# The opening of a diffusion trunk on one core: products of ones on TensorE, the first token half first in the DMA queue, another chain to the first norm, and both up-weights of block 1 as plain products

## The chip, the cores and the metric

One NeuronCore of a Trainium2 chip runs the whole program, in one launch. The engines are TensorE (PE, with its weight loads as PEld), VectorE (DVE), ScalarE (ACT), GpSimd (POOL) and SyncE (SP, whose queue issues most of the DMAs). The metric is the device time of one execution in microseconds (us); the time of a kernel is the median of several executions.

## The reference

One layer of a trunk on 640 tokens (512 latent, 128 context) of width 1024: half a SwiGLU feed-forward step, a token mixer (differential attention beside an mLSTM), and a second half feed-forward step. Each is preceded by an RMS norm whose scale and shift come from a conditioning vector (adaLN). The change touches only what comes first:

```python
def adaln(cvec, w, b):
    m = jax.nn.silu(cvec) @ w + b
    return m.reshape(cvec.shape[0], N_MOD, D_MODEL)

def swiglu(h, w1, w3, w2):
    return (jax.nn.silu(h @ w1) * (h @ w3)) @ w2

def layer(x, mods, l, p, ctx):
    m = [mods[:, j][:, None, :] for j in range(N_MOD)]
    g = p['g_norm'][l]
    hh = rmsnorm(x, g[0]) * (1 + m[1]) + m[0]
    x = x + 0.5 * m[2] * swiglu(hh, p['ffn1_w1'][l], p['ffn1_w3'][l], p['ffn1_w2'][l])
    ...
```

Everything is float32. D_FF is 2816, that is 11 blocks of 256 columns for `ffn1_w1` and `ffn1_w3`.

## The kernel before, in words

**Tiling.** Activations are kept transposed: 128 partitions x 8 slices d of the width x 640 tokens, and the tokens in two halves of 320 (half 0, half 1). A float32 product is made of three faster ones (`mm3`): weight and activation are each split into a high part, rounded to fp32r, and a low part, the remainder; high x high, high x low and low x high are added in PSUM. So a weight tile costs ACT a copy (the high part) and DVE a subtraction (the low part). A unit, 128 features x 320 tokens, is 8 slices x 3 = 24 matmuls of 128x320. Float32 matmuls that are not split show as two instructions each.

**Opening** (lines 751 to 919). `x` of half 0 is loaded in two parts (`load_x`), then the adaLN weights `w_ada_k` one k at a time (`start.load(k)`, 1 MB, four buffers, so that load k+4 waits for product k), and in between the weights W of block 0 in four pieces (`load_weights(i)`, `w1a` and `w3a`, slices 2i and 2i+1). `squares` squares x on ACT and DVE and adds pairs on DVE; `add_squares` sums over partitions by a matmul with `ones`; `rstd` and `refine` make the reciprocal root (`rv`, `rt`, `ry`; ACT does a logarithm and an exponential, DVE a Newton step). `product(k)` is a vector-matrix product of the conditioning with `w_ada_k` (16 matmuls into `ps_a`, a copy of the row to SBUF), `columns(k)` turns the row into columns (`ps_at`) and adds the bias and forms `scale`. `divide` multiplies x by the reciprocal root, `norm` applies scale and shift and splits the result into `hm`.

**First pass, second pass.** Then come 8 steps over k for half 0: step k makes 12 matmuls (two weights x two feature tiles x three products) into four accumulators (`ps_f`). Between its first 4 and the other 8 matmuls, `ahead` brings columns k+1, divide, norm of d=k+1 and the splits of W; behind the step stands product k+2. Squares, sum and `rstd` of half 1 are spread over steps 1 to 5. The second pass is 8 steps over half 1.

**Order.** In the opening each engine works as written (`keep_in_program_order`): PE, ACT, DVE and the DMAs on SP's queue each in the order of the program text. Behind the second pass a planner of the framework orders DVE and ACT by a simulated timeline, except where `tc.issue_after` binds an instruction to another one. PE stays in the order written. DMAs of one queue are issued in order, and an issue can wait for an earlier landing.

**Blocks 1 to 10.** A granule is one of `w1`, `w3` of one block. The first granule, `w1` of block 1, is computed plainly (`Whole`: `split` and 4 units, 96 matmuls). All others go through a seven-product scheme over 2x2 blocks (`Winograd.products`): 7 products of 4 slices x 3 matmuls, 84 in all, from sums of weights and of activations. `operand_sums` makes the activation sums once (S1 to S4, DVE and ACT; the low parts of S3 come by `third`, S4 by `fourth`). Per granule, `parts` makes weight parts (`wB`, `wC`, differences in `raw`) and `sums` splits what is left (`ww`). Raw weights have two buffers (`rawp`); the `w` ring for split weights has two. Products A22 and S4 of a granule are made during the next one. `modulation` hangs other work (column tiles of the rest of adaLN) on the granules by number.

Of the kernel before, what the change touches and what calls it, by code (L numbers as in the profile page):

```python
# [21 lines left out]
HALF = T // 2  # L22
# [9 lines left out]
def tile_trunk(ctx: ExitStack, tc: tile.TileContext, a: dict):  # L32
# [83 lines left out]
    cT = load(cp, [128, KT, 2], a["cT"], name="cT")  # L116
# [4 lines left out]
    for r in range(2):  # L121
        load_x(0, r)
    sel = cp.tile([128, 2], F32, name="sel")
# [123 lines left out]
    class Granule:  # L247
# [12 lines left out]
        def parts(self, fp):  # L260
# [12 lines left out]
            tt(vec, lo[:, nk:], lo[:, nk:], hi[:, nk:], ALU.subtract)  # L273
# [40 lines left out]
    class Winograd:  # L314
# [61 lines left out]
        def products(self, work, between, then=(), ahead=None, prepared=False, narrow=0):  # L376
# [356 lines left out]
    with ExitStack() as ph:  # L733
# [11 lines left out]
        class Opening:  # L745
# [8 lines left out]

            def squares(self, hf, r):
# [8 lines left out]
                tt(vec, p, p, q, ALU.add)  # L764
                self.sq[r] = p
                if r == 0:
                    order, psum.order = psum.order, [7]
                    self.ss[hf] = psum.tile([128, 512], F32, tag="mm", name="ps_ss")[:, :HALF]
                    psum.order = order

            def add_squares(self, hf, r):
                for i in range(2):
                    mm(self.ss[hf], ones, self.sq[r][:, i], start=r + i == 0, stop=r + i == 2)
# [14 lines left out]
            def divide(self, hf, r):  # L788
                xs = x_all[:, 2 * r : 2 * r + 2, half(hf)]
                tt(vec, xs, xs, self.rs[hf][:, None, :].to_broadcast([128, 2, HALF]), ALU.mult)  # L790

            def product(self, k):
# [9 lines left out]
                placed(vec.tensor_copy(self.row[k], ps[:, :256]))  # L802
# [32 lines left out]
        def split_weights(i, part):  # L835
            cs = slice(256 * PIECES[i][0], 256 * PIECES[i][1])
            for raw, (h, lo) in zip(raws, W):
# [93 lines left out]
        for k in range(KT):  # L931
# [5 lines left out]
            if k == 5:  # L937
                whole.split(t=[((0, 2048, w1[0]),), ((0, 1792, w1[1]), (1792, 2048, w1[2][:, :256]))])
# [10 lines left out]
        for f, hf in ((0, 1), (1, 1), (0, 0), (1, 0)):  # L949
            p = acc_tile(psum)  # L950
            for k in range(KT):
                mm3(p, whole.w(0, k, f), whole.w(1, k, f), *hs.hh(k, hf), k == 0, k == KT - 1)
            gate_first(f, hf, p, None)
# [1382 lines left out]
```

## Time and profile before

| | us |
|---|---|
| median of 3 executions | 1838.76 |
| lowest and highest | 1837.59, 1839.71 |
| profiled execution | 1840.36 |
| its span, first to last instruction | 1838.6 |

Mean granted TensorE clock of the profiled execution: 0.993 of full speed.

How to read it: a row of the timeline has start, duration, engine, line, operation, tiles (out<-in), shape and count, and in brackets the idle time of the engine before it with what ended it. Many instructions are made in helpers, so the line is that of the helper (75 for matmuls, 51 for ACT, 54 for DVE, 97 for DMAs) and the tile name tells what it is. The granted clock is what the throttle of TensorE allowed. The duration of a matmul in the profile is longer than its spacing from the next, since matmuls overlap. `128x320 f32` stands in the profile for fp32r matmuls too. SPq is SP's queue, on which DMAs are issued.

### The profile page before, as it was taken

How to read it: one execution, taken by the hardware profiler on the slowest of the kernel's cores; microseconds unless marked ns; L12 is line 12 of the kernel's file. 1: busy time of each engine (PE TensorE's matmuls, PEld its weight loads, DVE VectorE, ACT ScalarE, POOL GpSimd, SP SyncE). 2: the span in 40 equal slices, each digit the busy share in tenths (PEclk: the TensorE clock that was granted, in tenths of full speed). 3: DMA queues.
4: the chain of work that ended last, by engine and by line, in shares of the span. 5: the costliest groups of instructions: out<-in, count | busy, mean ns of one | idle time of the engine just before them, and what ended most of it. 6: DMA issues, size and time to landing. Idle time of an engine off the chain costs nothing.

```text
span 1838.6 us, 30679 instructions
## 1 busy us (share of the span) xinstructions
PE 1799.5 (98%) x12608; PEld 1761.4 (96%) x12608; DVE 1317.2 (72%) x2148; ACT 867.7 (47%) x1490; POOL 31.0 (2%) x55
## 2 busy tenths in 40 slices
PE   7999999999999999999999999999899999999999
PEld 5999999999999999999999999999899999999999
DVE  5898886577787757475585558876766878887575
ACT  4654454112655555454465555673235645554232
POOL 0000001110000000000000000000000000000000
PEclk8999999999999999999999999999999999999999
DMA  7354547975234322122222154574742345447872
GB/s 289 121 192 169 193 169 250 370 239 176 72 122 145 122 81 79 63 85 67 77 77 84 41 168 147 199 268 164 257 174 86 132 149 188 166 170 254 322 286 87
DMA packets 127709, 298.77 MB, mean 162 GB/s; under 512 B 9617, under 2 KB 90769, under 8 KB 114769
## 3 DMA queue, kind: packets, MB, share of 16 engines
q1 hardware_dynamic: 118306, 256.44, 40.1%
q0 software_dynamic: 9264, 40.37, 6.0%
q8 instruction: 99, 1.62, 0.4%
q14 instruction: 40, 0.33, 0.1%
HBM read 233.15 MB, written 63.63 MB: 161 GB/s over the span
## 4 chain that ended last, share of the span: by engine, by line
PE 84%; DVE 6%; DMA 5%; ACT 3%; issue 1%; SPq 0%; DVEq 0%; ACTq 0%
PE ps_f L75 45%; PE ps_p L75 16%; PE ps_t L75 11%; PE sc L75 3%; PE ps_o L75 2%; PE ps_n L75 2%; DMA ada<-csil_dram 2%; DVE ww L54 1%; PE ps_u L75 1%; PE ps_wT L78 1%; DMA raw_a<-in_w_ada_c 1%; PE ps_qkT L78 1%; DVE raw_a L716 1%; ACT wH L51 1%; PE ps_ss L75 1%
## 5 line engine op out<-in xcount | busy, mean ns | idle before, releaser
L75 PE MATMUL ps_f<-S,ww 128*128 128x320 f32 x2172 | 350.2, 310 | 5.8 <-DVE ww L54 4.2
L75 PEld LDWEIGHTS ps_f<-S,ww 128*128 128x128 f32 x2172 | 327.0, 189 | 8.5 <-DVE ww L54 6.9
L75 PE MATMUL ps_p<-hH,wH 128*128 128x320 f32 x672 | 213.4, 318 | 6.9 <-DVE y L54 6.2
L75 PE MATMUL ps_p<-hL,wH 128*128 128x320 f32 x672 | 208.2, 310 | 0.0
L75 PE MATMUL ps_p<-hH,wL 128*128 128x320 f32 x672 | 208.2, 310 | 0.0
L51 ACT ACTIVATE ww<-raw 128x2048 fp32r<-128x2048 f32 (+1 forms) x67 | 125.6, 1874 | 154.9 <-PE ps_f L75 87.6
L75 PE MATMUL ps_f<-hm,ww 128*128 128x320 f32 x1236 | 195.6, 311 | 2.5 <-DVE ww L54 2.5
L75 PEld LDWEIGHTS ps_f<-hm,ww 128*128 128x128 f32 x1236 | 185.8, 189 | 2.8 <-DVE ww L54 2.8
L75 PE MATMUL ps_t<-wH,hH 128*128 128x256 f32 x640 | 185.3, 289 | 0.9 <-DVE x L57 0.9
L75 PE MATMUL ps_t<-wH,hL 128*128 128x256 f32 x640 | 181.1, 283 | 0.9 <-DVE hL L54 0.9
L75 PE MATMUL ps_t<-wL,hH 128*128 128x256 f32 x640 | 180.9, 283 | 0.0
L54 DVE TENSOR_TENSOR ww<-raw,ww 128x2048 fp32r<-128x2048 f32 (+1 forms) x67 | 150.1, 2240 | 38.7 <-ACT ww L51 38.7
L75 PE MATMUL ps_f<-hm,wB 128*128 128x320 f32 x984 | 157.6, 309 | 0.0
L75 PEld LDWEIGHTS ps_f<-hm,wB 128*128 128x128 f32 x984 | 147.7, 188 | 0.0
L54 DVE TENSOR_TENSOR raw<-raw 128x1024 f32<-128x1024 f32 x159 | 137.6, 865 | 2.0
L75 PEld LDWEIGHTS ps_p<-hH,wH 128*128 128x128 f32 x672 | 126.9, 189 | 7.6 <-ACT wH L51 6.4
L75 PEld LDWEIGHTS ps_p<-hL,wH 128*128 128x128 f32 x672 | 126.9, 189 | 0.3
L75 PEld LDWEIGHTS ps_p<-hH,wL 128*128 128x128 f32 x672 | 126.7, 189 | 0.0
L54 DVE TENSOR_TENSOR wL<-raw,wH 128x2048 fp32r<-128x2048 f32 x43 | 98.3, 2286 | 35.6 <-ACT wH L51 35.6
L75 PEld LDWEIGHTS ps_t<-wH,hH 128*128 128x128 f32 x640 | 122.4, 191 | 1.5 <-ACT nsq L51 1.1
L75 PEld LDWEIGHTS ps_t<-wH,hL 128*128 128x128 f32 x640 | 122.4, 191 | 1.1 <-DVE hL L54 1.1
L75 PEld LDWEIGHTS ps_t<-wL,hH 128*128 128x128 f32 x640 | 122.5, 191 | 0.4
(303 smaller groups left out, 3353.7 us busy)
## 6 DMA issues: line engine op xcount, KB each, us to landing
g_dram<-g SPq DMA_DIRECT2D x44, 640.0 KB, 5.6
raw_a<-in_w_ada_c SPq DMA_DIRECT2D x24, 512.0 KB, 4.0
raw<-in_w1b SPq DMA_DIRECT2D x11, 1024.0 KB, 4.8
raw<-in_w3b SPq DMA_DIRECT2D x11, 1024.0 KB, 4.8
raw<-in_w1a SPq DMA_DIRECT2D x10, 1024.0 KB, 4.8
raw<-in_w3a SPq DMA_DIRECT2D x10, 1024.0 KB, 6.2
ada<-in_w_ada_c POOLq DMA_DIRECT2D x18, 512.0 KB, 5.0
hm<-g_dram POOLq DMA_DIRECT2D x7, 1280.0 KB, 10.5
```

The lines of the kernel that those rows point to most:

```text
L51: return placed(nc.scalar.activation(*args, **kw))
L54: return placed(eng.tensor_tensor(out=out, in0=in0, in1=in1, op=op))
L75: tc.keep_in_program_order(nc.tensor.matmul(*args, **kw))
L78: tc.keep_in_program_order(nc.tensor.transpose(*args, **kw))
L716: placed(vec.tensor_tensor_reduce(out=junk, in0=raw, in1=self.csil[:, v, :], op0=ALU.mult, op1=ALU.add, scale=1.0, scalar=0.0, accum_out=m ...
```

## The change

1. A method `keep_clock(n)` issues n matmuls of `ones` with `ones` (128x128, float32) into a PSUM bank that nothing reads; it is called with 14 ahead of everything else on PE, and with 3, 4 and 2 between the steps of the opening.
2. `cT`, the conditioning, is loaded by ACT's queue instead of SP's. On SP's queue W piece 0 goes ahead of load 0, x of half 1 goes behind load 5, and W pieces 2 and 3 go behind loads 4 and 6.
3. For half 0 the squares are not added in pairs across ACT and DVE: DVE adds its own two, and `ones` is multiplied with three tiles for each part instead of two.
4. W piece 0 is split ahead of `rstd`, the row of product 0 is copied by ACT, the first divide covers one slice of d only, and norm of d=0 goes ahead of product 1.
5. Squares of half 1 both stand behind step 3, their sums behind step 4, `refine` of half 1 in step 6.
6. `w3` of block 1 is computed plainly as well, from the `w` ring; the seven-product scheme begins at block 2. Parts of the second of its granules are bound ahead of `third`.

```diff
-    cT = load(cp, [128, KT, 2], a["cT"], name="cT")
+    cT = cp.tile([128, KT, 2], F32, name="cT")
...
+    nc.scalar.dma_start(out=cT, in_=a["cT"])
...
             if ahead is not None:
                 with tc.issue_after(work[0][0].split_at):
-                    behind = ahead()
+                    work[1][0].parts(self.fp)
+                with tc.issue_after(work[1][0].parts_at):
+                    ahead()
...
-                if not last:
-                    with tc.issue_after(behind if i == 0 and ahead is not None else gr.split_at):
+                if not last and (i > 0 or ahead is None):
+                    with tc.issue_after(gr.split_at):
                         work[i + 1][0].parts(self.fp)
...
+            def keep_clock(self, n):
+
+                if not hasattr(self, "idle"):
+                    self.idle = self.bank(3, "ps_idle")
+                for _ in range(n):
+                    mm(self.idle[:, :128], ones, ones, start=True, stop=True)
...
-                tt(vec, p, p, q, ALU.add)
-                self.sq[r] = p
+                if hf:
+                    tt(vec, p, p, q, ALU.add)
+                    self.sq[r] = p[:, 0], p[:, 1]
+                else:
+                    tt(vec, q[:, 0], q[:, 0], q[:, 1], ALU.add)
+                    self.sq[r] = p[:, 0], p[:, 1], q[:, 0]
...
-                placed(vec.tensor_copy(self.row[k], ps[:, :256]))
+                if k == 0:
+                    act(self.row[k], ps[:, :256], AF.Copy)
+                else:
+                    placed(vec.tensor_copy(self.row[k], ps[:, :256]))
...
         start = Opening()
+        load_weights(0)
         start.load(0)
         for t, n in ((sel, "sel"), (b_ada, "b_ada"), (g_norm, "g_norm")):
             dma(t, a[n])
-        load_weights(0)
         start.load(1)
         start.load(2)
-        load_x(1, 0)
         load_weights(1)
         start.load(3)
-        load_x(1, 1)
-        load_weights(2)
 
         psum.order = [4, 5, 6]
-        for r in range(2):
-            start.squares(0, r)
-            start.add_squares(0, r)
+        start.keep_clock(14)
+        start.squares(0, 0)
+        start.add_squares(0, 0)
+        start.squares(0, 1)
+        split_weights(0, "high")
+        split_weights(0, "low", slice(1))
+        start.add_squares(0, 1)
+        start.rstd(0)
+        split_weights(0, "low", slice(1, 2))
         start.product(0)
         start.load(4)
-        load_weights(3)
-        start.rstd(0)
-        split_weights(0, "high")
+        load_weights(2)
+        start.keep_clock(3)
         start.refine(0)
         start.columns(0)
-        start.divide(0, 0)
+        start.keep_clock(4)
+        start.divide(0, 0, 1)
+        start.norm(0, 0)
         start.product(1)
-        split_weights(0, "low")
-        start.norm(0, 0)
+        start.divide(0, 0, 1, 1)
         start.load(5)
+        load_x(1, 0)
+        load_x(1, 1)
+        start.keep_clock(2)
...
-                if k == 5:
+                if k == 6:
                     start.refine(1)
...
+                if k == 0:
+                    load_weights(3)
-            if k in (3, 4):
-                start.add_squares(1, k - 3)
-            if k in (1, 2):
-                start.squares(1, k - 1)
+            if k == 3:
+                for r in range(2):
+                    start.squares(1, r)
             if k == 4:
+                for r in range(2):
+                    start.add_squares(1, r)
                 start.rstd(1)
...
-        _, _, gate_first, _ = hs.work.pop(0)
-        whole = Whole(4, hs.up[0].fetch)
-        whole.load()
-        hs.up[1].load()
+        gated = [hs.work.pop(0)[2] for _ in range(2)]
+        whole = [Whole(4, gr.fetch) for gr in hs.up[:2]]
+        for w in whole:
+            w.load()
...
+        whole_units(whole[0], gated[0], ((0, 1), (1, 1), (0, 0), (1, 0)))
         with tc.issue_after(end.ins), tc.issue_after(at_act.ins):
             third, fourth = hs.operand_sums(lambda r: x_all[:, 2 * r : 2 * r + 2, :])
+        whole[1].split()
+        hs.up[3].load()
+        hs.store_g(hs.SO, 0)
+        whole_units(whole[1], gated[1], ((0, 0), (1, 0), (0, 1), (1, 1)))
         with tc.issue_after(end.ins), tc.issue_after(at_act.ins):
             hs.work[0][0].parts(fp)
             hs.work[0][0].sums()
-        hs.store_g(hs.SO, 0)
...
-                if (i, at) == (1, 1):
+                if (i, at) == (2, 1):
                     begin_columns()
-                if at and 2 <= i < 16:
+                if at and 3 <= i < 17:
                     columns.tile(hs.at_vec)
...
-        hs.run_whole(resid, half_m[:, 0], to_mixing, lambda i, at: modulation(i + 1, at), third)
+        hs.run_whole(resid, half_m[:, 0], to_mixing, lambda i, at: modulation(i + 2, at), third)
```

`whole_units` holds the loop of four units that stood in line before, `mm3` over 8 slices and then the gate. `bank` takes a PSUM tile from a named bank.

More of the change, by code (lines that the diff above doesn't have):

```diff
@@ L763, in squares @@
                 tt(vec, q, xs[:, 2:4], xs[:, 2:4], ALU.mult)
-                tt(vec, p, p, q, ALU.add)
-                self.sq[r] = p
+                if hf:
[4 more added lines that the diff above has]
+                    self.sq[r] = p[:, 0], p[:, 1], q[:, 0]
                 if r == 0:
-                    order, psum.order = psum.order, [7]
-                    self.ss[hf] = psum.tile([128, 512], F32, tag="mm", name="ps_ss")[:, :HALF]
-                    psum.order = order
+                    self.ss[hf] = self.bank(7, "ps_ss")[:, :HALF]
             def add_squares(self, hf, r):
-                for i in range(2):
-                    mm(self.ss[hf], ones, self.sq[r][:, i], start=r + i == 0, stop=r + i == 2)
+                sq = self.sq[r]
+                for i, t in enumerate(sq):
+                    mm(self.ss[hf], ones, t, start=r + i == 0, stop=r == 1 and i == len(sq) - 1)
             def rstd(self, hf):
@@ L786, in refine, with divide @@
                 self.rs[hf] = self.rs[hf][0]
[L788 to L790 removed]
+            def divide(self, hf, r, n=2, at=0):
+                xs = x_all[:, 2 * r + at : 2 * r + at + n, half(hf)]
+                tt(vec, xs, xs, self.rs[hf][:, None, :].to_broadcast([128, n, HALF]), ALU.mult)
             def product(self, k):
@@ L833, in load_weights, with split_weights @@
                 dma(raw[:, 256 * k0 : 256 * k1], src[:, k0:k1])
-        def split_weights(i, part):
+        def split_weights(i, part, which=slice(2)):
             cs = slice(256 * PIECES[i][0], 256 * PIECES[i][1])
-            for raw, (h, lo) in zip(raws, W):
+            for raw, (h, lo) in list(zip(raws, W))[which]:
                 if part != "low":
@@ L937, in tile_trunk @@
             if k == 5:
-                whole.split(t=[((0, 2048, w1[0]),), ((0, 1792, w1[1]), (1792, 2048, w1[2][:, :256]))])
+                whole[0].split(t=[((0, 2048, w1[0]),), ((0, 1792, w1[1]), (1792, 2048, w1[2][:, :256]))])
                 hs.up[2].load()
@@ L948, in tile_trunk, with whole_units @@
             hs.gate_plain(f, 1, (second[f, 0], second[f, 1]))
[L949 to L953, printed above, removed]
+        def whole_units(w, gate, order):
+            for f, hf in order:
+                p = acc_tile(psum)
+                for k in range(KT):
+                    mm3(p, w.w(0, k, f), w.w(1, k, f), *hs.hh(k, hf), k == 0, k == KT - 1)
+                gate(f, hf, p, None)
+        whole_units(whole[0], gated[0], ((0, 1), (1, 1), (0, 0), (1, 0)))
         with tc.issue_after(end.ins), tc.issue_after(at_act.ins):
             third, fourth = hs.operand_sums(lambda r: x_all[:, 2 * r : 2 * r + 2, :])
+        whole[1].split()
+        hs.up[3].load()
+        hs.store_g(hs.SO, 0)
+        whole_units(whole[1], gated[1], ((0, 0), (1, 0), (0, 1), (1, 1)))
         with tc.issue_after(end.ins), tc.issue_after(at_act.ins):
```

7 lines of the change are left out of this document (6 added, 1 removed).

## The prediction

> **What bounds the kernel now.** I read the page first, for the share of each engine and the slices of the span.
>
> ```profile
> span 1838.6 us, 30679 instructions
> PE 1799.5 (98%) x12608; PEld 1761.4 (96%) x12608; DVE 1317.2 (72%) x2148; ACT 867.7 (47%) x1490; POOL 31.0 (2%) x55
> PE   7999999999999999999999999999899999999999
> ```
>
> TensorE is the bound, and a gap elsewhere is worth little. The first slice (46 us) stands at 7, so I went on to windows of 3.41 us laid along the steps of the granted clock. Columns: stretch, its length, PE busy (instructions), granted clock, DMA share, GB/s.
>
> ```profile
> 6.91:10.33 3.42, 2.66 (x5) 1.00 0.99 352
> 10.33:13.74 3.41, 3.41 (x20) 1.00 1.04 401
> 13.74:17.15 3.41, 1.96 (x25) 1.00 0.99 403
> 17.15:20.57 3.42, 1.32 (x6) 0.50 1.07 405
> 20.57:23.98 3.41, 3.41 (x17) 0.50 1.02 380
> 27.39:30.81 3.42, 3.42 (x21) 0.50 1.06 420
> 30.81:34.22 3.41, 3.41 (x40) 1.00 1.00 413
> 47.87:51.29 3.42, 2.29 (x19) 1.00 0.42 139
> 92.25:95.66 3.41, 0.70 (x3) 1.00 0.00 0
> 95.66:99.07 3.41, 3.05 (x11) 0.50 0.58 211
> ```
>
> The clock changes at the ends of such windows. After one with PE busy for 1.96 us or 0.70 us it is halved, after one with 2.29 us it is not. It was half from 17.15 to 30.81, while the first pass ran. DMA is at its limit meanwhile, about 400 GB/s.
>
> Then the timeline of the opening (start, duration, engine, operation; in brackets the idle time before it and what ended it).
>
> ```profile
> 5.85 0.74 ACT L51 ACTIVATE sq<-x 128x640 f32<-128x640 f32 x1 [1.91 <-DMA x<-in_x]
> 7.67 4.63 PE L75 MATMUL ps_ss<-sq,ones 128*128 128x320 f32 x8 [7.67 <-DVE sq L54]
> 12.23 1.79 PE L75 MATMUL ps_a<-raw_a,small 128*32 128x256 f32 x16
> 14.44 0.48 DVE L63 TENSOR_SCALAR rv<-ps_ss 128x320 f32<-128x320 f32 x1
> 15.50 1.07 PE L75 MATMUL ps_a<-raw_a,small 128*32 128x256 f32 x16 [0.32 <-DMA raw_a<-in_w_ada_k]
> 17.01 0.49 DVE L57 SCALAR_TENSOR_TENSOR ry<-rt,ry 128x320 f32<-128x320 f32 x1
> 17.69 0.82 DVE L54 TENSOR_TENSOR x<-x,ry 128x640 f32<-128x640 f32 x1
> 18.54 0.65 ACT L51 ACTIVATE hm<-x,mod,scale 128x320 fp32r<-128x320 f32 x1 [1.57 <-DVE x L54]
> 19.25 1.44 PE L75 MATMUL ps_f<-hm,wH 128*128 128x320 f32 x4 [2.67 <-ACT hm L51]
> ```
>
> The recorded clock says 1.00 up to 17.15, but product(0) took 1.79 us at 12.23 and product(1), the same 16 matmuls, 1.07 us at 15.50: PE starts at half speed, and the first record of 1.00 is no measurement of that. The first pass starts at 19.25, sent off by the chain from `ps_ss` over `rv` and `ry` to `hm`.
>
> Last, the one place where PE stands still before the steady part, found as the drop at 92.25 above, and the two stretches around its end (PE, PEld, DVE, ACT, POOL, clock, DMA share, GB/s):
>
> ```profile
> 79.33 1.90 ACT L51 ACTIVATE ww<-raw 128x2048 fp32r<-128x2048 f32 x1
> 83.59 0.33 SPq L97 DMA_DIRECT2D raw<-in_w3a  x1
> 89.93 0.63 ACT L51 ACTIVATE wC<-raw 128x512 fp32r<-128x512 f32 x1 [2.35 <-DMA raw<-in_w3a]
> 91.74 1.90 ACT L51 ACTIVATE ww<-raw 128x2048 fp32r<-128x2048 f32 x1
> 93.67 2.29 DVE L54 TENSOR_TENSOR ww<-raw,ww 128x2048 fp32r<-128x2048 f32 x1 [0.78 <-ACT ww L51]
> 96.02 3.04 PE L75 MATMUL ps_f<-S,ww 128*128 128x320 f32 x10 [1.77 <-DVE ww L54]
> ```
>
> ```profile
> 92.40:96.02 3.62, 0.56 (x3) 0.30 (x3) 2.84 (x3) 1.57 (x2) 0.00 (x0) 0.95 0.00 0
> 96.02:99.07 3.05, 3.05 (x11) 3.05 (x12) 3.05 (x4) 1.47 (x2) 0.00 (x0) 0.50 0.65 236
> ```
>
> ACT runs in order: `wC` waits for weights issued at 83.59, `ww` stands behind it, and the seven-product matmuls of the next granule wait for its low half.
>
> **The change part by part.** Prices at full clock, from the chain of waits (start, duration, work), from windows of all engines, from the page's DMA issues (size, us to landing) and from groups of instructions between 67.4 and 92.4 (busy, mean ns):
>
> ```profile
> 40.82 0.34 PE ps_at L75 x4
> 42.43 1.00 PE ps_a L75 x16
> 43.44 1.29 PE ps_ss L75 x4
> 53.20:67.40 14.20, 14.20 (x98) 14.20 (x98) 13.73 (x32) 11.08 (x21) 0.00 (x0) 1.00 0.17 62
> 67.40:81.50 14.10, 14.10 (x99) 14.10 (x98) 12.31 (x18) 9.40 (x15) 0.00 (x0) 1.00 0.18 71
> raw_a<-in_w_ada_k SPq DMA_DIRECT2D x8, 1024.0 KB, 10.8
> x<-in_x SPq DMA_DIRECT2D x4, 640.0 KB, 7.8
> L54 DVE TENSOR_TENSOR raw<-raw 128x512 f32<-128x512 f32 (+1 forms) x6 | 5.2, 862 | 0.0
> L54 DVE TENSOR_TENSOR wB<-raw,wB 128x1024 fp32r<-128x1024 f32 x2 | 2.4, 1218 | 0.0
> L54 DVE TENSOR_TENSOR wC<-raw,wC 128x512 fp32r<-128x512 f32 x2 | 1.4, 684 | 0.0
> ```
>
> The second pass's 96 matmuls take 14.20 us, 0.148 each, so a step of 12 takes 1.78 us, a product 1.00, a columns 0.34, and an `ones` product (two instructions) 0.64. The first pass ends at 53.20.
>
> *Landings.* cT leaves SP's queue: x is issued first and, by that slot, about 0.45 us earlier; ACT, which issues cT now, is idle until x lands at 5.85. At 404 GB/s a product's weights (1024 KB) take 2.6 us, half a token half (640 KB) 1.6, a piece of W (by the code two of 256 KB) 1.3. Up to product(1)'s weights the same bytes are sent in another order; they landed at 15.50, now 15.05. Loads 4 and 5 wait on SP for products 0 and 1, with W piece 2 and x behind them, but four loads are then still under way. Behind them in the new order, W piece 1 ahead of the weights of product(3): product(2) 17.7, (3) 21.6, (4) 24.2, W piece 2 25.5, (5) 28.1, x of half 1 at 29.7 and 31.3, (6) 33.9, W piece 3 35.2, (7) 37.8. The second half of x is moved past two loads of weights: the squares of half 1, now both at step 3, wait on ACT and DVE for it until 31.3 and hold the mod, scale and norm of d=5 behind them until 33.9 (two rounds of 0.83 on DVE, then 0.65 of ACT). That costs nothing while PE itself waits for product(6)'s weights until 33.9; without that cover it would cost up to 2.7 us.
>
> *Fillers.* 14 products of ones from about 1.0 us, 28 instructions. No 128x128 f32 matmul of that kind is in the trace: by the nearest rows one costs between 0.085 (`ps_at`, two columns) and 0.32 (`ps_ss`, 320 columns), doubled at half clock. I take 128/320 of the latter, 0.13, 0.26 cold, since columns set the pace there. So they end between 6.3 and 8.3; the squares are ready at 6.2. The 9 later ones (18 instructions, 2.3 us) stand mostly in waits.
>
> *To the first norm.* The sum of squares becomes 6 products, 12 instructions of 0.32: 3.9 us, from 7.3 in the middle to 11.2, or 12.2. From the start of `rv` to the first matmul it was 4.81 us; one 320-wide divide of 0.49 instead of 0.82 leaves 4.5: 15.7 to 16.7. In PE's order product(1) and two fillers stand ahead: 15.05 + 1.00 + 0.5 = 16.6. The first pass starts 2.65 us earlier. Copying row 0 on ACT costs nothing (ACT is free between the exponential and the norm), 0.4 us without that.
>
> *First pass.* Steps 0 to 4 with products 2 to 5: 5 x 1.78 + 4 x 1.00 + 5 x 0.34 = 14.6, to 31.2. PE waits for product(6) until 33.9. Then 1.0 for it, 2.6 for the sums of half 1 behind it, step 5 2.1, product(7) 1.0, step 6 2.1, step 7 1.8: 44.5. The refine of half 1 (three of 0.49) and a divide now come ahead of the last low half on DVE, which is late by 0.8: 45.3. That is 7.9 us before 53.20.
>
> *The clock on the way.* 2.7 us idle within one window leave PE 0.7 us, as at 92.25; split over two they leave about 2.05, between the 1.96 and the 2.29 above. I expect one window at half clock, 3.41 us worth 1.7. The opening then gives 6.2 us. A rule speaks for none: the Trainium skill, TensorE: Matmul & The Clock Gate, section Why this matters for your kernels, asks that PE not idle more than about 3 us between bursts. The trace is stricter: no gap in 13.74:17.15 reaches 3 us and the clock fell.
>
> *Block 1.* Four units of 8 x 3 matmuls instead of seven products of 4 x 3: 96 for 84, 12 more, +1.78 us. The stall goes: of the 3.62 us to 96.02 PE worked for two or three matmuls of 0.148, 3.25 lost, and up to 99.07 it did eleven instead of 20.6, 1.4 more: -4.65. The next in line is not late: the raw weights it waited for are now loaded behind the plain split, some 14 us before the first seven-product matmul, and DVE has 28 us for what it did in 14 to 16, plus one low half of 2.29, minus a whole granule's parts and sums. Putting the second granule's parts ahead of the low S3 uses 4.5 us of that slack on DVE (half of 5.2 + 2.4 + 1.4); they are needed four products later. Numbers passed to the modulation move by one because one granule fewer is in the list; each column tile keeps its place.
>
> *Sum* against the profiled execution's 1840.36 (its span 1838.6 and 1.8 around it): -6.2 - 4.65 + 1.78 = -9.1, 1831.3. That execution is 1.60 above the median of 1838.76, so 1829.7 for the median.
>
> **The rivals.** *The clock does not dip* at product(6), 20 in 100: 1828.0. That is what the rule quoted would give. For it: the gap may fall across two windows; against it: 2.05 is nearer to 1.96.
>
> *The second plain weights are split late,* 15: in the 14.10 us of the first plain granule DVE was busy for 12.31, and a split of this size began on ACT 11.9 us in (79.33) and ended on DVE at 83.56, 16.2 in. Put there again it would end 2.1 us late: 1831.8. Against it: the 4.5 us of a granule's parts no longer stand ahead of it.
>
> *The stall moves,* 13: ACT's order again puts parts that wait for a transfer ahead of the split that PE needs, one granule later. The whole 4.65 come back: 1834.4. For it: nothing in the edit changes who orders ACT there. Against it: weights now arrive one granule ahead.
>
> *The fillers do not lift the clock,* 10, the slower side: 20.57:23.98 shows PE busy for the whole window and the clock still halved after it, so busy time is not all that counts. Then they are 28 x 0.26 in front of sums that take 12 x 0.58 cold (4.63 for 8): 15.3, then product(0) 1.8, fillers and columns 4.3, product(1) 1.8, two fillers 1.0, 24.2 for the first step, 4.95 later than before. With -4.65 + 1.78 that is +2.1: 1840.8. It decides from about 3 us of PE time that the fillers cost on the path. At the upper price of a filler, 0.64 cold, the first 28 last until 18.9, and it would be 10.6 more. The Trainium skill, same page, section Part 1: The HAM clock gate, has one busy window of 3.4 us release the clock; by it this rival would be out, but 20.57:23.98 disagrees.
>
> **How the numbers follow.** Forecast 1829.7, 38 in 100; the rivals 20, 15, 13 and 10; 4 for a price that I have not thought of, above. This kernel can tell 0.2% (3.7 us) from no change: faster means under 1835.1. The first four cases lie under it, less 2 for two of them together: 0.84. The fillers' rival at its middle price is within 0.2%: same 0.11; at its upper price, with what is left over, slower 0.05. The range starts at 1826.0: no dip, and half of the 2.8 us recovered that the first pass could still gain if only product(7)'s weights bound it (37.8 + 1.0 + 2.1 + 1.8 = 42.7 for 45.3). It ends at 1835.0, above the moved stall.
>
> **What would show it.** Granted clock 1.00 at the first `ps_f`, which starts near 16.6; product(6) released by DMA near 34; one window at 0.50 near there; second pass starting near 45 to 47; no PE gap over 1 us where the seven-product matmuls begin, near 89, and no clock drop there; 12 more `ps_f` matmuls. A first step after 19, or a `ww` that PE waits for in block 2, makes the forecast wrong.

## The result and the profile after

| | before | after |
|---|---|---|
| median of 7 executions each, us | 1838.20 | 1832.19 |
| lowest and highest | 1836.37, 1839.71 | 1831.40, 1832.81 |
| profiled execution | 1840.36 | 1832.00 |
| its span | 1838.6 | 1830.2 |
| its mean granted clock | 0.993 | 0.997 |

The ratio is 0.9964, 95% interval 0.9954 to 0.9973: 6.0 us faster, where 9.1 were forecast. The time lies inside the range. In the page of the changed kernel the first slice of PE has gone from 7 to 8:

```profile
span 1830.2 us, 30782 instructions
...
PE   8999999999999999999999999999899999999999
```

The windows of 3.41 us, laid along the clock's steps (columns: stretch, length, then busy time and instructions of PE, PEld, DVE, ACT, POOL, then granted clock, DMA share, GB/s):

```profile
7.78:11.19 3.41, 1.90 (x7) 1.06 (x6) 2.33 (x5) 2.17 (x4) 0.00 (x0) 1.00 1.06 418
...
14.60:18.02 3.42, 3.42 (x36) 2.60 (x35) 1.67 (x6) 1.31 (x2) 0.00 (x0) 1.00 1.02 405
31.67:35.08 3.41, 1.84 (x24) 1.33 (x22) 3.27 (x6) 1.36 (x2) 0.00 (x0) 1.00 1.05 411
```

No window of the opening is at half clock, neither from 17 us on, where four of them stood before, nor behind 35.08, where one was forecast. The timeline of the opening of the changed kernel (start, duration, engine, operation; in brackets the idle time before it and what ended it):

```profile
1.05 4.95 PE L75 MATMUL ps_idle<-ones 128*128 128x128 f32 x28 [1.05 <-DVE ones L128]
6.03 3.66 PE L75 MATMUL ps_ss<-sq,ones 128*128 128x320 f32 x12
11.80 1.07 PE L75 MATMUL ps_a<-raw_a,small 128*32 128x256 f32 x16 [2.12 <-DMA raw_a<-in_w_ada_k]
13.94 1.14 PE L75 MATMUL ps_idle<-ones 128*128 128x128 f32 x8
14.12 0.16 DVE L54 TENSOR_TENSOR mod<-ps_at,b_ada 128x4 f32<-128x4 f32 x1 [1.32 <-PE ps_at L75]
14.91 0.65 ACT L51 ACTIVATE hm<-x,mod,scale 128x320 fp32r<-128x320 f32 x1 [1.59 <-DVE x L54]
15.01 1.07 PE L75 MATMUL ps_a<-raw_a,small 128*32 128x256 f32 x16
16.48 0.83 PE L75 MATMUL ps_f<-hm,wH 128*128 128x320 f32 x4
19.98 0.85 PE L75 MATMUL ps_f<-hm,wH 128*128 128x320 f32 x4
23.41 0.85 PE L75 MATMUL ps_f<-hm,wH 128*128 128x320 f32 x4
34.34 1.07 PE L75 MATMUL ps_a<-raw_a,small 128*32 128x256 f32 x16 [1.57 <-DMA raw_a<-in_w_ada_k]
45.27 2.91 PE L75 MATMUL ps_f<-hm,wH 128*128 128x320 f32 x18 [0.59 <-DVE hm L54]
```

The sum of squares is done at 9.69, but product(0) waits 2.12 us for its weights, and DVE waits for the columns made from it (`mod` at 14.12). The first step begins at 16.48 (before: 19.25), with product(1) and fillers right ahead of it. A step with its product lasts 3.43 us (19.98 to 23.41). PE waits 1.57 us for the weights of product(6).

Block 1 of the changed kernel: windows of the two plain granules, and the timeline from the first seven-product matmuls to the next wait of PE.

```profile
45.85:60.04 14.19, 14.19 (x98) 14.19 (x98) 13.72 (x32) 10.22 (x20) 0.00 (x0) 1.00 0.07 18
60.04:74.10 14.06, 14.06 (x98) 14.06 (x97) 13.03 (x16) 10.32 (x16) 0.00 (x0) 1.00 0.37 146
```

```profile
88.20 1.92 PE L75 MATMUL ps_f<-hm,wB 128*128 128x320 f32 x12
89.96 3.68 PE L75 MATMUL ps_f<-S,ww 128*128 128x320 f32 x24
97.52 0.35 SPq L97 DMA_DIRECT2D csil<-in_c_rows  x1
106.11 1.91 ACT L51 ACTIVATE csil<-csil 128x2048 f32<-128x2048 f32 x1 [1.39 <-DMA csil<-in_c_rows]
...
108.40 2.02 PE L75 MATMUL ps_f<-S,ww 128*128 128x320 f32 x12 [0.68 <-ACT u L51]
```

PE is busy throughout both plain granules, and the stall of 92.40 to 99.07 has no successor. Twenty us later a small one appears: ACT's `csil` (silu of the conditioning for the column tiles) waits for a transfer issued at 97.52, `u` stands behind it, and PE waits 0.68 us for `u`.

To see how the 8.4 us between the two spans come about, the same matmuls are compared in both timelines: the first of the token mixer (`ps_t`) and two of the second feed-forward. Before:

```profile
485.26 0.36 PE L75 MATMUL ps_t<-wH,hH 128*128 128x256 f32 x1 [0.86 <-DVE x L57]
1465.54 1.92 PE L75 MATMUL ps_f<-S,ww 128*128 128x320 f32 x12
1465.59 1.06 ACT L51 ACTIVATE wB<-raw 128x1024 fp32r<-128x1024 f32 x1 [0.55 <-PE ps_f L75]
1466.56 1.90 ACT L51 ACTIVATE ww<-raw 128x2048 fp32r<-128x2048 f32 x1
1470.83 1.73 PE L75 MATMUL ps_f<-S,ww 128*128 128x320 f32 x10 [1.32 <-DVE ww L54]
1472.40 0.90 PE L75 MATMUL ps_f<-hm,ww 128*128 128x320 f32 x5
```

After:

```profile
475.41 0.36 PE L75 MATMUL ps_t<-wH,hH 128*128 128x256 f32 x1 [0.86 <-DVE x L57]
1457.90 1.92 ACT L51 ACTIVATE ww<-raw 128x2048 fp32r<-128x2048 f32 x1
1458.34 1.92 PE L75 MATMUL ps_f<-S,ww 128*128 128x320 f32 x12
1459.72 1.04 ACT L51 ACTIVATE wB<-raw 128x1024 fp32r<-128x1024 f32 x1
1461.86 2.07 PE L75 MATMUL ps_f<-S,ww 128*128 128x320 f32 x12
1463.76 0.46 PE L75 MATMUL ps_f<-hm,ww 128*128 128x320 f32 x2
```

The lead is 9.85 us at `ps_t`, 7.20 at the `ps_f<-S,ww` of 1465.54, and 8.64 a few matmuls on. The step of 1.4 us there was not forecast: before, ACT makes `wB` ahead of the split `ww`, and PE waits 1.32 us for the low half of `ww`; after, ACT makes `ww` first and the wait is gone. That the lead shrinks by 2.65 us in between is no effect of the change as far as the runs show: from the first `ps_t` to the end of the span the fourteen profiles of this study took between 1352.6 and 1356.9 us, the kernel before 1353.3 and 1355.3, the changed one 1354.8, 1354.3 and 1356.7.

### The profile page after: what moved, and what is told of

The parts are those of the page before. It is cut to its first block, busy times and chain, and to the rows that moved or that the text cites. A ratio compares the mean times of both kernels' runs of the same rounds, so it can differ in the third digit from the quotient of the medians.

```text
span 1830.2 us, 30782 instructions
## 1 busy us (share of the span) xinstructions
PE 1801.2 (98%) x12670; PEld 1764.9 (96%) x12670; DVE 1312.0 (72%) x2141; ACT 865.7 (47%) x1486; POOL 30.9 (2%) x55
## 4 chain that ended last, share of the span: by engine, by line
PE 84%; DVE 6%; DMA 6%; ACT 3%; issue 1%; SPq 0%; ACTq 0%; DVEq 0%
PE ps_f L75 45%; PE ps_p L75 16%; PE ps_t L75 11%; PE sc L75 3%; PE ps_o L75 2%; PE ps_n L75 2%; DMA raw_a<-in_w_ada_k 1%; PE ps_u L75 1%; PE ps_wT L78 1%; DVE ww L54 1%; DMA ada<-csil_dram 1%; DMA so<-o_dram 1%; PE ps_qkT L78 1%; DMA raw_a<-in_w_ada_c 1%; DVE wL L54 1%
## 5 line engine op out<-in xcount | busy, mean ns | idle before, releaser
L75 PE MATMUL ps_f<-S,ww 128*128 128x320 f32 x2136 | 343.4, 310 | 1.7 <-ACT u L51 0.7
L75 PEld LDWEIGHTS ps_f<-S,ww 128*128 128x128 f32 x2136 | 320.9, 188 | 4.3 <-DVE ww L54 3.2
L75 PE MATMUL ps_f<-hm,ww 128*128 128x320 f32 x1320 | 207.6, 310 | 2.6 <-DVE ww L54 2.6
L75 PEld LDWEIGHTS ps_f<-hm,ww 128*128 128x128 f32 x1320 | 197.6, 188 | 3.1 <-DVE ww L54 2.8
L75 PE MATMUL ps_f<-hm,wB 128*128 128x320 f32 x960 | 153.8, 309 | 0.0
```

Source lines behind the costliest of these rows:

```text
L75: tc.keep_in_program_order(nc.tensor.matmul(*args, **kw))
```

## The experiments

All of them in one table. "Under before" is the difference of the medians within one group of runs, on one chip. The next three columns are of the profiled execution: start of the first step (`ps_f`), start of block 1 (the first matmul with `wgA`), and half-clock windows before 40 us + between 80 and 100 us. The last is the mean granted clock over all executions; those of before, 69 in the three groups, have 0.9940.

| run | median, us | under before | ratio, 95% interval | first step | block 1 | windows | clock |
|---|---|---|---|---|---|---|---|
| before, as predicted from | 1838.20 | | | 19.25 | 67.55 | 4 + 1 | |
| after | 1832.19 | 6.0 | 0.9964, 0.9954 to 0.9973 | 16.48 | 60.04 | 0 + 0 | 0.9964 |
| e1 before again | 1839.11 | 0.6 | 0.9995, 0.9986 to 1.0004 | 18.71 | 64.87 | 2 + 1 | 0.9941 |
| e2 after again | 1831.93 | 7.7 | 0.9960, 0.9944 to 0.9975 | 16.20 | 60.18 | 0 + 0 | 0.9964 |
| e3 block 1 only | 1835.46 | 4.2 | 0.9977, 0.9967 to 0.9987 | 18.49 | 63.34 | 2 + 0 | 0.9949 |
| e4 opening only | 1835.43 | 4.2 | 0.9975, 0.9963 to 0.9987 | 16.18 | 59.82 | 0 + 1 | 0.9956 |
| e5 no fillers | 1833.18 | 6.7 | 0.9965, 0.9952 to 0.9979 | 16.33 | 59.74 | 0 + 0 | 0.9953 |
| e6 fillers only | 1837.94 | 1.9 | 0.9993, 0.9983 to 1.0003 | 17.11 | 65.69 | 2 + 1 | 0.9954 |
| e7 x of half 1 early | 1832.27 | 7.6 | 0.9964, 0.9950 to 0.9977 | 16.23 | 61.00 | 0 + 0 | 0.9967 |
| e8 two waits removed | 1829.47 | 10.4 | 0.9947, 0.9934 to 0.9960 | 16.61 | 59.33 | 0 + 0 | 0.9964 |
| e9 chain only | 1837.89 | 2.0 | 0.9987, 0.9977 to 0.9996 | 15.59 | 62.47 | 2 + 1 | 0.9943 |
| e10 order only | 1839.60 | 0.3 | 0.9996, 0.9986 to 1.0006 | 17.99 | 62.95 | 2 + 1 | 0.9946 |
| e11 after, third time | 1833.65 | 6.3 | 0.9963, 0.9951 to 0.9976 | 16.38 | 60.49 | 0 + 0 | 0.9963 |
| e12 two waits removed again | 1831.37 | 8.6 | 0.9950, 0.9936 to 0.9964 | 16.30 | 59.03 | 0 + 0 | 0.9962 |

**Both kernels again** (e1, e2: no edit).

> The kernel before, unchanged, profiled once more. Theory A (the difference between 9.9 us at the start of block 2 and 6.0 in the medians is the state that an execution falls into: the profiled one had four windows at half clock in the opening, 17.15 to 30.81): this execution has another phase of the clock windows; if it has three in the opening instead of four, the second pass starts near 51.5 instead of 53.2 and the span is near 1836.5. Rival B (the opening is the same in every execution and the rest is given back behind 1170 us): four windows again, second pass at 53.2, span within 1 us of 1838.6.

> The changed kernel, unchanged, profiled once more. Both theories: second pass at 45.9 within 0.5 us, no half-clock window before 340 us, span 1830 to 1831.5. The wait of ACT for `so` at 1226, 1.83 us in the first profile and none in the profile of before: if it is a transfer's chance it is gone or differs by more than 0.5 us, and the stretch from 1073 to 1287 is up to 1.8 us shorter; if it belongs to the change it is there again at 1.8.

The kernel before, profiled again, has two half-clock windows in the opening (19.33 to 26.16) where its first profile had four, and block 1 begins 2.7 us earlier with the same instructions. So the profile that the prediction was made from was a poor one of its kind just where the sum was made. The theory of e1 holds for the opening, but its span is only 0.8 us shorter (1837.8), as the rival had it: from the first `ps_t` to the end it takes 2.0 us more (1355.3 for 1353.3). The changed kernel has none in any of three profiles; its wait for product(6) was 1.57, 1.96 and 2.10 us. ACT's wait for `so`, which e2 asked about, is 1.83, 1.44 and 0.93 us in them and 0.75 in e1, so it is not the change's; the span of e2, 1828.9, lies under the 1830 to 1831.5 expected.

**The two halves of the change** (e3, e4).

```diff
 # e3: the kernel before, with item 6 of the change alone
-        whole = Whole(4, hs.up[0].fetch)
+        whole = [Whole(4, gr.fetch) for gr in hs.up[:2]]
...
+                    work[1][0].parts(self.fp)
+                with tc.issue_after(work[1][0].parts_at):
+                    ahead()
 # e4: the kernel before, with items 1 to 5 alone
```

> Before with the block-1 part alone (both weights plain, opening as before). Theory: second pass at about 53 as before, no PE gap over 1 us and no half-clock window between 80 and 130, and behind it 2.5 us earlier than before (4.65 of stall away, 1.78 of matmuls added, 0.4 for the 0.68 us wait for csil that came with it): median about 2.5 under before. Rival (the stall was the price of late weights behind the opening and moves on): a gap of 3 us and a half-clock window reappear one granule later, median 1.8 over before.

> The changed opening alone, block 1 as before (one plain weight). Theory: second pass at 45.9, so 7.4 us earlier than in the first profile of before; the stall of 3.3 us and its half-clock window come again, now near 85 to 91; median 3.5 to 5.5 under before. Rival (an earlier opening only runs into the same transfer of the second granule's weights): the stall grows by what the opening gained, median within 1 us of before.

Each half gives 4.2 us, and together 8.4, where the whole change gave 7.7 in the same group. In e4 the stall of block 1 stands where it stood, a gap of 1.77 us behind one of 0.86, and with it the half-clock window; ten matmuls take 3.02 us, where twelve take 1.92 at full clock:

```profile
86.14 0.55 PE L75 MATMUL ps_f<-S,ww 128*128 128x320 f32 x2 [0.86 <-ACT ww L51]
88.47 3.02 PE L75 MATMUL ps_f<-S,ww 128*128 128x320 f32 x10 [1.77 <-DVE ww L54]
```

e3 gives 1.3 us more than the 2.87 (4.65 less 1.78) of the prediction, but its interval, 2.4 to 6.1 us, holds 2.87 too. One gain that was not forecast is in the timeline of e3 at the second feed-forward:

```profile
1462.08 1.92 ACT L51 ACTIVATE ww<-raw 128x2048 fp32r<-128x2048 f32 x1
1463.91 1.04 ACT L51 ACTIVATE wB<-raw 128x1024 fp32r<-128x1024 f32 x1
```

`products` serves both feed-forwards, so binding the parts of the second granule ahead of `third` changed ACT's order there too. The gap of 1.31 or 1.32 us stands in all six profiles without item 6 (before, e1, e4, e6, e9, e10) and in none of the eight with it. e3 has the new wait for `csil` as well, 1.30 us, which takes back as much as the second feed-forward gains:

```profile
110.03 1.91 ACT L51 ACTIVATE csil<-csil 128x2048 f32<-128x2048 f32 x1 [2.01 <-DMA csil<-in_c_rows]
112.32 1.88 PE L75 MATMUL ps_f<-S,ww 128*128 128x320 f32 x11 [1.30 <-ACT u L51]
```

Matmul by matmul, e3 leads the first profile of before by 4.21 us at the start of block 1, by 7.48 at 118 us, by 6.29 behind the wait for `csil`, and by 3.02 and 4.45 ahead of and behind the place in the second feed-forward. So block 1 itself gives 3.27, or 3.64 against e1, for 2.87; the rest of the 1.3 is not explained.

**The fillers** (e5: the change without them; e6: the kernel before with them).

```diff
 # e5
-        start.keep_clock(14)
...
-        start.keep_clock(3)
...
-        start.keep_clock(4)
...
-        start.keep_clock(2)
 # e6: the same four calls added to the kernel before, with keep_clock
```

> The changed kernel without its 23 filler products; nothing else differs in the opening. Theory (the fillers lift the clock at the end of the first window and hold it): at half speed the sums of squares take 12 x 0.53 = 6.4 us from about 6.2, so the first step is sent off by them at 17 to 18 instead of 16.3, one or two windows at half clock follow in the opening, product(6) does not wait for its weights, and the second pass starts 1.5 to 4 us later than 45.9. Median 1 to 4 over the changed kernel. Rival (the end of the first pass is set by the transfers, which land product(6)'s weights at 34.2 and product(7)'s near 37.6 whatever the clock): second pass at 46 to 46.5, median within 0.5 of the changed kernel.

> The kernel before with the fillers alone (14, 3, 4 and 2, at the like places), everything else as before. Theory (the clock is most of what the opening gains): no half-clock window before 80, first step at 16.5 to 17.5, first plain granule at 60.5 to 62 instead of 63.3 to 67.6, the stall near 87 to 92 unchanged; median 2.5 to 4.5 under before, most of what the whole opening gave (4.2). Rival (order and chain give the gain): first step at 18.5 or later, first plain granule after 63, median within 1 of before.

The theory that the fillers give the gain fell. Without them the first step begins at 16.33, as with them, and PE goes on with product(6)'s weights at 34.03, for 34.34 with fillers, as the rival had it. The timeline of e5 shows why:

```profile
5.99 5.82 PE L75 MATMUL ps_ss<-sq,ones 128*128 128x320 f32 x12 [5.99 <-ACT sq L51]
11.75 1.07 PE L75 MATMUL ps_a<-raw_a,small 128*32 128x256 f32 x16
...
16.33 0.85 PE L75 MATMUL ps_f<-hm,wH 128*128 128x320 f32 x4 [0.81 <-ACT hm L51]
```

The cold sum takes 5.82 us instead of 3.66, and ends 2.1 us later. But product(0) starts at 11.75 without fillers, right behind the sum, and at 11.80 with them, since its weights land at 11.76; in the first profile of before they landed at 10.27, with load 0 ahead of W piece 0. DVE works in order, so the norm needs the columns of product(0) as well as the root. With fillers the root is done at 12.79 and waits for them, so `hm` is ready at 15.56 (14.91 + 0.65), only 0.7 us earlier than in e5 (16.27). PE then makes nothing of these 0.7: it is busy with product(1) and fillers until 16.48, where e5 waits for `hm` until 16.33.

The mean clock over executions is higher with fillers, 0.9964 for 0.9953 with the rest of the change and 0.9954 for 0.9940 without it; 0.0011 and 0.0014 of some 1835 us would be 2.0 and 2.6 us. That the fillers do this in the opening is not shown: the one profile of e5 has no half-clock window there either, and its two more than the changed kernel's first profile begin at 348.6 and 1014.2. The time shows less: e5 lies 6.7 us under before, the changed kernel 6.0, 7.7 and 6.3, so what the fillers are worth net there is not to be told from nothing, and alone they give 1.9 with an interval that holds 0. In e6 the early start runs into the old order of transfers:

```profile
17.11 0.85 PE L75 MATMUL ps_f<-hm,wH 128*128 128x320 f32 x4 [0.20 <-ACT hm L51]
23.93 1.07 PE L75 MATMUL ps_a<-raw_a,small 128*32 128x256 f32 x16 [0.92 <-DMA raw_a<-in_w_ada_k]
29.56 1.12 PE L75 MATMUL ps_a<-raw_a,small 128*32 128x256 f32 x16 [2.13 <-DMA raw_a<-in_w_ada_k]
```

PE waits for products whose weights stand behind x of half 1, and the clock falls at 30.45 instead of about 17.

**The chain and the order, each alone** (e9, e10, neither with fillers).

```diff
 # e9: the kernel before, with items 3 and 4, cT on ACT's queue and W piece 0 ahead of load 0
+        start.squares(0, 1)
+        split_weights(0, "high")
...
+        start.divide(0, 0, 1)
+        start.norm(0, 0)
         start.product(1)
 # e10: the kernel before, with items 2 and 5
         start.load(5)
+        load_x(1, 0)
+        load_x(1, 1)
```

> The kernel before with the shorter chain alone: three tiles of squares, W piece 0 issued ahead of load 0 and split ahead of the root, row 0 copied by ACT, a divide of one slice, the norm of d=0 ahead of product(1), and cT on ACT's queue. No fillers; x of half 1, W pieces 2 and 3, the squares and sums of half 1 and block 1 as before. Theory: what the opening gives is the idle time of 2.7 us ahead of the first step that the shorter chain takes away; first `ps_f` near 16.3, no half-clock window or one before 40 us, first plain `wgA` at 61 to 62, the time 2.5 to 4 us under the kernel before. Rival: the chain alone gives little, because the order of the transfers behind it decides when the pass runs; then `wgA` is not before 63 and the time lies within 1.5 us of the kernel before.

> The kernel before with the order of the transfers alone: cT on ACT's queue, W piece 0 ahead of load 0, x of half 1 behind load 5, W pieces 2 and 3 behind loads 4 and 6, and squares, sums and refine of half 1 at their later steps. Old chain to the first norm, no fillers, block 1 as before. Theory: PE stays idle for about 2.5 us ahead of the first step, first `ps_f` at 18.3 to 19, half-clock windows (two or more) before 40 us, `wgA` at 62.5 to 66, the time 0 to 2 us under the kernel before. Rival: the order alone gives the gain of the opening; then `wgA` is near 60 and the time 3.5 us or more under the kernel before.

Neither the theory nor the rival of e9 came out whole: the first step came even earlier than expected, 15.59, the gap ahead of it is all but gone, yet two half-clock windows followed and block 1 began at 62.47; the time is 2.0 under, between the two. e10 went as its theory said, but for a first step 0.3 us earlier: the wait of 2.62 us for `hm` is still there,

```profile
17.99 1.43 PE L75 MATMUL ps_f<-hm,wH 128*128 128x320 f32 x4 [2.62 <-ACT hm L51]
```

two windows at half clock follow, and the time is 0.3 under, which can't be told from nothing. Chain 2.0, order 0.3 and fillers 1.9 add up to the 4.2 of e4, but that is no proof that they add: only the chain's interval leaves 0 out, e9 and e10 both hold cT on ACT's queue and W piece 0 ahead of load 0, and with chain and order together the fillers gave nothing that shows. How the opening's gain divides among its parts stays open. One profile each of e4 and e5, in which chain and order stand together, has no window at half clock.

**x of half 1 earlier, and the two small waits** (e7, e8, e11, e12).

```diff
 # e7: the change, with x of half 1 behind loads 2 and 3 again
         start.load(2)
+        load_x(1, 0)
         load_weights(1)
         start.load(3)
+        load_x(1, 1)
...
         start.load(5)
-        load_x(1, 0)
-        load_x(1, 1)
 # e8 and e12: the change, with the second part of x of half 1 behind load 6
-        load_x(1, 1)
...
                 if k == 0:
+                    load_x(1, 1)
                     load_weights(3)
-            if k == 3:
-                for r in range(2):
-                    start.squares(1, r)
...
+            if k in (3, 4):
+                start.squares(1, k - 3)
...
+                if (i, at) == (4, 0):
+                    with tc.issue_after(hs.at_copy.ins):
+                        act(box["csil"], box["csil"], AF.Silu)
```

e8 and e12 are the same kernel. In it the sums of half 1 also stand a step later, ahead of product(7), and the column tiles begin one granule later.

> The changed kernel with x of half 1 loaded where it was before (behind loads 2 and 3) instead of behind load 5. Theory (all transfers ahead of product(6) stay the same bytes, only steps 1 to 3 see their weights later): products 3 and 4 wait for transfers, 1 to 3 us together, product(6) still starts at 34.2, and the first plain granule starts at 60 within 0.5: median within 0.7 of the changed kernel. Rival (the new place is what feeds the first steps): first plain granule 1.5 to 3 us later.

> The changed kernel with the second part of x of half 1 behind load 6, its squares behind step 4, the sums of half 1 behind step 5 ahead of product(7), and csil's silu bound behind a copy u on ACT. Theory: product(6)'s weights land 1.6 us earlier, the 1.6 to 2.0 us wait for them goes, the first plain granule starts near 58.4 instead of 60.1, and the gap of 0.7 to 1.2 us at 108 goes: median 1.5 to 2.5 under the changed kernel. Rival (DVE then is the bound of steps 4 to 6: two rounds of squares stand ahead of the norms): first plain granule at 59.5 to 60.5, median within 1.

> The changed kernel unaltered, beside the next run on one chip. Both theories: 6 to 8 us under the kernel before.

> The changed kernel with the second part of x of half 1 behind load 6, its squares at step 4, and ACT's silu of the conditioning bound behind a later copy, once more. Theory: the two small waits that the change opened (for product(6), and ACT's wait for the conditioning in block 2) cost about 2 us together; 1.5 to 3 us under the changed kernel. Rival: what the earlier run showed was the spread of executions; within 1 us of the changed kernel.

In e7 the one wait for product(6) became three, of 1.26, 0.76 and 0.29 us, for products (3), (4) and (5), and block 1 began at 61.00, later than the theory's 60 within 0.5 and earlier than the rival's 61.5; the time is that of the changed kernel. The place of x moves the wait for transfers rather than removing it. In e8 and e12 both waits are gone. In the timeline of e12, products (6) and (7) start without one, and `csil` comes once PE no longer waits behind it:

```profile
32.54 1.07 PE L75 MATMUL ps_a<-raw_a,small 128*32 128x256 f32 x16
38.86 1.07 PE L75 MATMUL ps_a<-raw_a,small 128*32 128x256 f32 x16
108.31 1.92 PE L75 MATMUL ps_f<-hm,wB 128*128 128x320 f32 x12
108.90 1.91 ACT L51 ACTIVATE csil<-csil 128x2048 f32<-128x2048 f32 x1
328.08 0.56 PE L75 MATMUL ps_f<-hm,ww 128*128 128x320 f32 x2 [2.31 <-ACT ww L51]
```

Block 1 begins at 59.33 and 59.03, earlier than in the changed kernel (60.04 to 60.49) but not at the 58.4 that e8 expected. And the version brought a wait of its own, the last line: near 328 us PE stands still twice, 2.31 and 1.77 us (e8: 2.06 and 1.77), with half clock behind it, where the three profiles of the changed kernel have one gap of 2.56 to 3.06 us near 345. What moved it was not tested.

The version beat the changed kernel by 2.3 us on the same chip (1831.37 against 1833.65), within the 1.5 to 3 of its expectation. The intervals of e11 and e12 overlap, but e8 gave the same sign in another group, 0.9947 beside e7's 0.9964. It is the fastest of the kernels here.

## Why the prediction was right, and where it was off

*The first step* came at 16.48 for 16.6, and product(6)'s weights let PE go on at 34.34 for about 34. The transfers were worked out nearly: product(1)'s weights release it at 14.45 in e5, for 15.05. The path to 16.6 was another than the one forecast. Product(1) started at 15.01 because fillers stood ahead of it, not because its weights came then, so it is luck that this time agrees with 15.05. The prediction also had no term for product(0)'s weights, for whose columns the first norm waited 1.32 us, and the later fillers did not stand mostly in waits: `hm` was ready 0.92 us before PE got to the first step. Nor does a warm sum carry the gain: e5 reaches the same first step with most of the sum cold.

*The fillers' price* was sized well: in the changed kernel their starts lie 0.21 us apart cold and 0.11 warm, for 0.26 and 0.13, and the first 28 took 4.95 us. The rival of the slower side is out: the sum behind them ran at full speed, 3.66 us for 12.

*The first pass* was sized with a row of the second. A step with product takes 3.43 us, not 3.12. Its matmuls mostly start 0.147 us apart, as forecast, but three times in a step, behind the product, behind the columns and ahead of the next product, it is 0.23 to 0.25, which makes 0.28 of the 0.31. So PE reached product(6) 1.6 us later (32.77, that is 34.34 - 1.57, for 31.2) and waited 1.57 for 2.7. The end of the pass hangs on those weights, and so it came near: the second pass begins at 45.85, forecast were 45.3 without a dip of the clock and 47 with one.

*The clock at product(6)* did not fall: the rival of no dip, at 20 in 100, is what happened, in every profile of the change. The window held 1.84 us of PE work, under the 1.96 that had been taken for a bound.

*Block 1.* The stall went and did not move, the second plain weights were in time, and the 12 more matmuls cost about their price (60.04 to 74.10 for 98 instructions). By medians the half gave 4.2 for 2.87, with an interval that holds both; by the profiles of e3 block 1 itself gave 3.3 to 3.6. Two things were missed that nearly cancel in e3: the same edit removed 1.3 us from the second feed-forward, since the prediction had not followed it into `products`, and the new wait for `csil`, 0.68 us here and 1.17 in e2, was not foreseen: the prediction let the column tiles keep their places, and did not follow the silu that stands ahead of them on ACT, whose transfer came 8.6 us after its issue (97.52 to 106.11).

*The sum* is where the miss arose. Against the profiled execution it gave 1831.3, and the profiled execution after took 1832.0. That this is so near is in part luck: the lead at the start of block 1 was 7.5 us for the 6.2 of the opening, since the clock did not dip, and 2.65 us that no term held went the other way behind the first `ps_t`. The last step, taking 1.60 off because the execution of before lay that far above its median, could not stand beside that sum: the 6.2 us of the opening were measured from an opening with four windows at half clock, and the change removes them. What was unusual in that opening was counted as gain, and the distance of the same execution from its median was then taken off as if the changed kernel had it too. In e1 the opening has two such windows and is 2.7 us shorter. By medians the opening is worth 4.2 us for 6.2, the term that fits worst, though the interval of e4, 2.4 to 6.8, does not exclude 6.2. In profiles block 1 begins at 67.55, 64.87 and 63.34 with the old opening (before, e1, e3) and at 59.82 to 60.49 with the new one (after, e2, e4, e11): 2.9 to 7.7 us earlier, in the mean 5.1. The two halves make 8.4, the whole made 6.0, 7.7 and 6.3 in three comparisons; intervals of 3 to 6 us width leave open whether something of the parts is lost where they stand together. The lower end of the range has a slip: 42.7 for 45.3 is 2.6 us, not 2.8, and half of it under 1828.0 gives 1826.7.

How much of the gain is clock can be estimated from the means: 0.9964 - 0.9940 is 0.0024 of 1836 us, at most 4.4 of the 6 to 7.7 us, and less where PE would have waited at full clock too. One window of 3.41 us at half clock costs up to 1.7 us, 0.0009 of the span; e3, which removes the one of block 1, has just that much more than before (0.9949). The profiles agree: the kernel before has five and three such windows ahead of 100 us and the changed one none, and behind 340 us it has three and three, the changed one three, two and three.

## What to carry to other kernels

Sum a change against two or three profiles of the kernel before when the clock falls in the stage concerned: what one profile shows of it may be its worst case, and a distance to the median must not be taken off again where the change removes what made it. Filling an engine's idle time is worth what the next wait lets through: look at which of chain, queue and transfers is last once the first of them is faster, and change them together. When an edit lies in a helper, list every place that calls it and read the profile there too.

## What the runs showed of the hardware

PE's busy time in a window did not decide whether the clock fell after it. Four windows at full clock, of e9, of e5 (both with the window that follows), of e11 and of e1:

```profile
12.75:16.16 3.41, 2.29 (x28) 1.51 (x24) 2.00 (x6) 1.63 (x3) 0.00 (x0) 1.00 0.98 402
16.16:19.58 3.42, 2.84 (x12) 2.46 (x12) 2.28 (x6) 1.03 (x3) 0.00 (x0) 0.50 1.08 395
```

```profile
14.12:17.54 3.42, 2.08 (x22) 1.07 (x21) 1.94 (x7) 1.31 (x2) 0.00 (x0) 1.00 1.03 411
17.54:20.95 3.41, 3.07 (x30) 2.29 (x31) 2.36 (x7) 2.00 (x4) 0.00 (x0) 1.00 1.02 422
```

```profile
33.10:36.51 3.41, 1.73 (x19) 1.06 (x20) 2.60 (x7) 2.10 (x4) 0.00 (x0) 1.00 0.91 360
```

```profile
12.50:15.91 3.41, 2.41 (x36) 1.25 (x36) 1.30 (x3) 1.46 (x4) 0.00 (x0) 1.00 1.01 425
```

After 2.29 us of work the clock was halved, after 2.08, 1.73 and 2.41 it was not. The kind of matmul does not sort these rows either. In the window of e9 most of the work was matmuls of product and columns (`128*32`, `128x2`), and in those of e5 and e11 a sum or a step of 320 columns had a larger share; but the window of e1 held product and columns alone, and the clock stayed (its two half-clock windows begin at 19.33). Of later windows with 320-column matmuls alone, those with 1.65 us of work (e6, from 91.89) and 1.68 (e1, from 350.42) were followed by half clock, and one with 1.61 (e2, from 344.21) was not. What decides stays open.

The first record of the clock marks where it is lifted. In the changed kernel it begins at 4.36, and the fillers start 0.21 us apart until 4.20 and 0.11 from 4.39 on; in e5 it begins at 10.71, and the matmuls of the sum start 0.53 us apart until 10.41 and 0.27 from 10.83 on. Ahead of it nothing is recorded, so a 1.00 shown there is no reading. For the kernel before that holds up to 13.74, and the slow product(0) at 12.23 begins ahead of the record, not against it. With fillers the first record begins at 4.36 to 6.99 (eight profiles), without them at 9.33 to 13.74 (six): the fillers do lift the clock early in every profile, whatever that is worth behind them.

The steps of the clock keep a grid of 3.41 us that starts elsewhere in each execution: the first record lies at 4.36, 6.29 and 5.80 us in three profiles of the changed kernel. So the same gaps fall into one window or across two, and the kernel before lost two windows of its opening in one profile and four in another.
